# One SBUF ring with large tapering loads, fp32 exp in place and one activation table set in a log-sum-exp kernel

## The chip, the cores and the metric

The kernel runs on one core of a Trainium2 chip. The metric is the device time of the program in microseconds (us), as the median of several runs. The profile of one execution gives a span, from the first to the last instruction; the device time of the same run is longer, by the time outside the span.

## The reference

```python
def setup_inputs():
    batch, seq, dim = 32, 512, 1024
    return {"x": np.random.randn(batch, seq, dim).astype(np.float32), "axis": -1}

def reference(x, axis):
    x_max = np.max(x, axis=axis, keepdims=True)
    return (x_max.squeeze(axis) + np.log(np.sum(np.exp(x - x_max), axis=axis))).astype(np.float32)
```

There are 16,384 rows of 1,024 fp32 numbers, 67.11 MB, and one result per row. Both kernels leave the maximum out, because for normally distributed numbers exp does not overflow. They put 128 consecutive rows on each of the 128 partitions. From here on a "row" is one row on every partition: 128 x 4 KB = 0.524 MB. There are 128 of them.

## The kernel before

Separate pools hold tiles of 4, 2 and 1 rows. ScalarE makes bf16 exponentials in a second tile and VectorE sums them. Some rows are "fused": ScalarE writes exp and its accumulator gives the sum, without VectorE.

```python
SCHEDULE = [(4, 24), (2, 8), (1, 16)]      # rows per tile, number of tiles: 48 loads
N_TAIL_FUSED = 4
X_BUFS = {4: 4, 2: 4, 1: 6}
E_BUFS = {4: 3, 2: 3, 1: 4}
SCALAR_FUSE_EVERY = 2
# ... cut: pools, views ...
            xt = xpools[r].tile([P, r, D], fp32, name=f"xt{r}")
            nc.sync.dma_start(out=xt, in_=x_views[r][t])                 # L75
            if r == 1 and m0 >= NB - N_TAIL_FUSED:
                nc.scalar.activation(out=xt[:, 0], in_=xt[:, 0], func=Exp,
                                     accum_out=sums[:, m0 : m0 + 1])     # L78
            else:
                # ... cut: one fused row (L91) in every second tile of 4 ...
                et = epools[r].tile([P, r, D], bf16, name=f"et{r}")
                nc.scalar.activation(out=et[:, j0:r], in_=xt[:, j0:r], func=Exp)   # L98
                nc.vector.reduce_sum(out=sums[:, m0 + j0 : m0 + r],
                                     in_=et[:, j0:r], axis=mybir.AxisListType.X)   # L99
# ... cut ...
    nc.scalar.activation(out=res, in_=sums, func=Ln)                     # L107
    nc.scalar.dma_start(out=out_v, in_=res)
```

The softmax here doesn't subtract the row's maximum and nothing guards it: scores larger than these inputs give would overflow.

Of the kernel before, what the change touches and what calls it, by code (L numbers as in the profile page):

```python
# [1 line left out]

# [4 lines left out]


SCHEDULE = [(4, 24), (2, 8), (1, 16)]  # L10
N_TAIL_FUSED = 4
X_BUFS = {4: 4, 2: 4, 1: 6}
E_BUFS = {4: 3, 2: 3, 1: 4}
SCALAR_FUSE_EVERY = 2


@with_exitstack
def kernel(
    ctx: ExitStack,
    tc: tile.TileContext,  # L20
    x: bass.AP,
    axis: bass.AP,
    out: bass.AP,
):
    nc = tc.nc
    P = nc.NUM_PARTITIONS

    assert axis in (-1, len(x.shape) - 1), f"only last-axis reduction supported, got {axis}"

    x_flat = x.flatten_outer_dims()  # L30
    N, D = x_flat.shape
    assert N % P == 0
    NB = N // P

    fp32 = mybir.dt.float32
    bf16 = mybir.dt.bfloat16
    Exp = mybir.ActivationFunctionType.Exp
    Ln = mybir.ActivationFunctionType.Ln

    assert sum(r * c for r, c in SCHEDULE) == NB, "schedule must cover all blocks"  # L40

    out_v = bass.AP(
        tensor=out.tensor,
        offset=out.offset,
        ap=[[NB, P], [1, NB]],
    )

    sizes = sorted({r for r, _ in SCHEDULE})
    xpools = {}
    epools = {}  # L50
    for r in sizes:
        xpools[r] = ctx.enter_context(
            tc.tile_pool(name=f"xpool{r}", bufs=X_BUFS.get(r, 4))
        )
        epools[r] = ctx.enter_context(
            tc.tile_pool(name=f"epool{r}", bufs=E_BUFS.get(r, 4))
        )
    spool = ctx.enter_context(tc.tile_pool(name="spool", bufs=1))
    opool = ctx.enter_context(tc.tile_pool(name="opool", bufs=1))

    sums = spool.tile([P, NB], fp32)

    x_views = {
        r: x_flat.rearrange("(p t j) d -> t p j d", p=P, t=NB // r, j=r) for r in sizes
    }

    block = 0
    big_tile_idx = 0
    for r, count in SCHEDULE:
        for _ in range(count):  # L70
            m0 = block
            t = m0 // r
            assert m0 % r == 0
            xt = xpools[r].tile([P, r, D], fp32, name=f"xt{r}")
            nc.sync.dma_start(out=xt, in_=x_views[r][t])  # L75

            if r == 1 and m0 >= NB - N_TAIL_FUSED:
                nc.scalar.activation(  # L78
                    out=xt[:, 0],
                    in_=xt[:, 0],  # L80
                    func=Exp,
                    accum_out=sums[:, m0 : m0 + 1],
                )
            else:
                j0 = 0
                if r >= 4:
                    fuse_one = (big_tile_idx % SCALAR_FUSE_EVERY) == 0
                    big_tile_idx += 1
                    if fuse_one:
                        j0 = 1  # L90
                        nc.scalar.activation(  # L91
                            out=xt[:, 0],
                            in_=xt[:, 0],
                            func=Exp,
                            accum_out=sums[:, m0 : m0 + 1],
                        )
                et = epools[r].tile([P, r, D], bf16, name=f"et{r}")
                nc.scalar.activation(out=et[:, j0:r], in_=xt[:, j0:r], func=Exp)  # L98
                nc.vector.reduce_sum(  # L99
                    out=sums[:, m0 + j0 : m0 + r],  # L100
                    in_=et[:, j0:r],
                    axis=mybir.AxisListType.X,
                )
            block += r

    res = opool.tile([P, NB], fp32)
    nc.scalar.activation(out=res, in_=sums, func=Ln)  # L107
    nc.scalar.dma_start(out=out_v, in_=res)


# [1 line left out]
_INS = ['x', 'axis']  # L112
_OUTS = [((32, 512), 'float32')]
#: Inputs that are plain numbers.
_NUMBERS = {'axis': -1}


# [26 lines left out]
```

## Time and profile before

| quantity | before |
|---|---|
| device time on the first chip, median of 4 | 169.53 us (169.18 to 170.11) |
| device time on the three other chips, median of 7 each | 168.66, 168.59, 168.59 us |
| span of the profiled run | 166.7 us |
| loads of x | 48 |
| ScalarE / VectorE busy | 74% / 75% |
| last load landed / last Ln ended | 161.42 / 164.27 us |

The page of the profile begins with the busy time of the engines, then cuts the span into 40 slices, in tenths of busy time, and then gives the chain of work that ended last and the costliest groups:

```profile
span 166.7 us, 278 instructions
...
DVE 124.3 (75%) x44; ACT 124.0 (74%) x79; POOL 0.2 (0%) x4
...
DMA  5999999999999999999999999999999999999940
GB/s 193 440 433 436 429 413 433 436 433 429 421 421 436 436 433 429 405 436 436 433 429 409 436 436 433 429 417 425 425 415 425 425 411 418 409 409 409 407 186 16
...
q1 hardware_dynamic: 6912, 67.11, 95.9%
...
q14 instruction: 2, 0.02, 0.0%
...
DMA 78%; ACT 17%; SPq 2%; issue 1%; ACTq 0%
```

The DMA row is full from the second slice on, and 78% of the last chain are loads. Both compute engines are three quarters busy, but they wait for data. So the stream of loads is what has to become shorter.

The timeline of ScalarE shows the pace. Its columns are start, duration, engine, line, operation, output and input, shapes, count; the brackets hold the idle time before and what ended it. These are three tiles of 4 rows, then two of 1 row later on ("..." stands for lines left out):

```profile
32.57 3.62 ACT L98 ACTIVATE et<-xt 128x4096 bf16<-128x4096 f32 x1 [1.15 <-DMA xt<-in_x_dram]
37.40 1.06 ACT L91 ACTIVATE xt<-xt 128x1024 f32<-128x1024 f32 x1 [1.22 <-DMA xt<-in_x_dram]
...
42.36 3.62 ACT L98 ACTIVATE et<-xt 128x4096 bf16<-128x4096 f32 x1 [1.16 <-DMA xt<-in_x_dram]
...
151.26 1.06 ACT L98 ACTIVATE et<-xt 128x1024 bf16<-128x1024 f32 x1 [0.22 <-DMA xt<-in_x_dram]
152.54 1.06 ACT L98 ACTIVATE et<-xt 128x1024 bf16<-128x1024 f32 x1 [0.22 <-DMA xt<-in_x_dram]
```

ScalarE waits for every tile, so the distances are those of the loads: about 4.89 us for 4 rows, or 1.22 a row, and 1.28 for a single row. Small tiles cost more per row. (The landings in the trace give the line: 0.078 us per load plus 1.202 to 1.204 us per row.)

The end of the same timeline:

```profile
161.50 1.06 ACT L78 ACTIVATE xt<-xt 128x1024 f32<-128x1024 f32 x1
162.47 0.19 ACT L78 ACTIVATION_READ_ACCUMULATOR xt<-xt 128x1 f32 x1
162.67 1.28 ACT L107 ACT_TABLE_LOAD   x1
163.96 0.31 ACT L107 ACTIVATE res<-sums 128x128 f32<-128x128 f32 x1
164.30 0.37 ACTq L108 DMA_DIRECT2D out_dram<-res  x1
```

After the last load has landed (161.42, from the semaphore records of the trace) there are 2.85 us to the end of Ln. A table load of 1.28 us stands in them, because exp and Ln are taken from two table sets.

### The profile page before, as it was taken

To read this page: it belongs to the slowest core of one execution; us is meant where nothing else is said; L and a number is where in the kernel's file an instruction comes from. 1 tells how busy PE (TensorE), PEld (TensorE's weight loads), DVE (VectorE), ACT (ScalarE), POOL (GpSimd) and SP (SyncE) were. 2 spreads that over 40 slices of the span, in tenths; PEclk is the share of its full clock that TensorE was granted. 3 is DMA by queue.
4 is the path that set the end of the run, shared out by engine and by line. 5 is a ranking of instruction groups with operands and counts; after the bars stand their busy time and mean duration, and the time that the engine had idled before them with its cause. 6 is when DMAs were issued, how large, how long until landed. Compare 5 with 4: busy or idle time off the path is not lost.

```text
span 166.7 us, 278 instructions
## 1 busy us (share of the span) xinstructions
DVE 124.3 (75%) x44; ACT 124.0 (74%) x79; POOL 0.2 (0%) x4
## 2 busy tenths in 40 slices
DVE  0016986868798686879868687886869999999930
ACT  3088777778877777977777797777798787978894
POOL 0000000000000000000000000000000000000000
DMA  5999999999999999999999999999999999999940
GB/s 193 440 433 436 429 413 433 436 433 429 421 421 436 436 433 429 405 436 436 433 429 409 436 436 433 429 417 425 425 415 425 425 411 418 409 409 409 407 186 16
DMA packets 7058, 67.19 MB, mean 403 GB/s; under 512 B 784, under 2 KB 912, under 8 KB 2960
## 3 DMA queue, kind: packets, MB, share of 16 engines
q1 hardware_dynamic: 6912, 67.11, 95.9%
q10 hardware_dynamic: 144, 0.07, 0.1%
q14 instruction: 2, 0.02, 0.0%
HBM read 67.11 MB, written 0.07 MB: 403 GB/s over the span
## 4 chain that ended last, share of the span: by engine, by line
DMA 78%; ACT 17%; SPq 2%; issue 1%; ACTq 0%
DMA xt<-in_x_dram 78%; ACT et L98 16%; SPq L75 2%; ACT xt L78 1%; ACT L107 1%; ACT res L107 0%; ACTq L98 0%; ACTq L78 0%
## 5 line engine op out<-in xcount | busy, mean ns | idle before, releaser
L99 DVE TENSOR_REDUCE sums<-et 128x3 f32<-128x3072 bf16 (+3 forms) x44 | 124.3, 2863 | 35.5 <-ACT et L98 35.5
L98 ACT ACTIVATE et<-xt 128x3072 bf16<-128x3072 f32 (+3 forms) x44 | 103.9, 2369 | 19.5 <-DMA xt<-in_x_dram 19.2
L91 ACT ACTIVATE xt<-xt 128x1024 f32<-128x1024 f32 x12 | 12.7, 1056 | 19.5 <-DMA xt<-in_x_dram 19.5
L78 ACT ACTIVATE xt<-xt 128x1024 f32<-128x1024 f32 x4 | 4.2, 1056 | 0.5 <-DMA xt<-in_x_dram 0.2
L91 ACT ACTIVATION_READ_ACCUMULATOR xt<-xt 128x1 f32 x12 | 2.2, 187 | 0.0
L91 ACT ACT_TABLE_LOAD x1 | 1.3, 1283 | 0.7 <-PEq L125 0.7
L107 ACT ACT_TABLE_LOAD x1 | 1.3, 1283 | 0.0
L78 ACT ACTIVATION_READ_ACCUMULATOR xt<-xt 128x1 f32 x4 | 0.7, 186 | 0.0
L107 ACT ACTIVATE res<-sums 128x128 f32<-128x128 f32 x1 | 0.3, 309 | 0.0
L125 POOL MEMSET const-bfloat16-1.0<- 128x1 bf16 x1 | 0.1, 102 | 0.0
L125 POOL MEMSET const-uint8-127<- 128x1 uint8 x1 | 0.1, 102 | 0.0
L125 POOL MEMSET const-float32-0.0<- 128x1 f32 x1 | 0.1, 99 | 0.2 <-issue 0.2
L125 POOL MEMSET const-float32-1.0<- 128x1 f32 x1 | 0.1, 99 | 0.0
## 6 DMA issues: line engine op xcount, KB each, us to landing
xt<-in_x_dram SPq DMA_DIRECT2D x24, 2048.0 KB, 15.8
xt<-in_x_dram SPq DMA_DIRECT2D x8, 1024.0 KB, 13.0
xt<-in_x_dram SPq DMA_DIRECT2D x16, 512.0 KB, 6.6
out_dram<-res ACTq DMA_DIRECT2D x1, 64.0 KB, 1.6
```

What stands on the lines that cost most here:

```text
L75: nc.sync.dma_start(out=xt, in_=x_views[r][t])
L78: nc.scalar.activation(out=xt[:, 0], in_=xt[:, 0], func=Exp, accum_out=sums[:, m0 : m0 + 1],)
L91: nc.scalar.activation(out=xt[:, 0], in_=xt[:, 0], func=Exp, accum_out=sums[:, m0 : m0 + 1],)
L98: nc.scalar.activation(out=et[:, j0:r], in_=xt[:, j0:r], func=Exp)
L99: nc.vector.reduce_sum(out=sums[:, m0 + j0 : m0 + r], in_=et[:, j0:r], axis=mybir.AxisListType.X,)
L107: nc.scalar.activation(out=res, in_=sums, func=Ln)
L125: nc = _bacc.Bacc("TRN2", target_bir_lowering=False, num_devices=1)
```

## The change

The intent is to move the same bytes in fewer, larger loads, to drop the bf16 tiles so that there is room for one ring of 50 rows (200 KB on each partition), to divide the sums between ScalarE's accumulator and VectorE, and to take exp and Ln from one table set. The core of the diff, with cuts:

```diff
-SCHEDULE = [(4, 24), (2, 8), (1, 16)]
+CHUNKS = [                         # rows of the load, rows of it that VectorE sums
+    (12, 4), (14, 4), (16, 4), (16, 9), (16, 11), (12, 8), (10, 6), (8, 5),
+    (6, 4), (5, 3), (4, 2), (3, 1), (2, 0), (2, 0), (1, 0),
+]
+LAST_PARTS = [512, 512]
+RING_ROWS = 50
...
+    ring = pool.tile([P, RING_ROWS, D], fp32, name="ring")
+    nc.scalar.preload_act_table_set("natural_log_exp_and_others")
...
+    for r, n_dve in CHUNKS:
+        if slot + r > RING_ROWS:
+            slot = 0
+        nc.sync.dma_start(out=ring[:, slot : slot + r], in_=x_v[:, row : row + r])
+        if n_dve:
+            nc.scalar.activation(out=ring[:, slot : slot + n_dve],
+                                 in_=ring[:, slot : slot + n_dve], func=Exp)      # L60
+            nc.vector.reduce_sum(out=sums[:, row : row + n_dve],
+                                 in_=ring[:, slot : slot + n_dve], axis=AX)       # L63
+        for j in range(n_dve, r):
+            nc.scalar.activation(out=ring[:, slot + j], in_=ring[:, slot + j],
+                                 func=Exp, accum_out=sums[:, row + j : row + j + 1])  # L67
...
+    # last row: two loads of 512 columns, two fused halves (L84), after the first
+    # half Ln of the other 127 rows (L92), then a sum of the two parts on VectorE (L93)
+    # and Ln of one row (L94)
```

More of the change, by code (lines that the diff above doesn't have):

```diff
@@ L7 @@
 from concourse._compat import with_exitstack
-SCHEDULE = [(4, 24), (2, 8), (1, 16)]
-N_TAIL_FUSED = 4
-X_BUFS = {4: 4, 2: 4, 1: 6}
-E_BUFS = {4: 3, 2: 3, 1: 4}
-SCALAR_FUSE_EVERY = 2
+CHUNKS = [
[4 more added lines that the diff above has]
+RING_ROWS = 50
 @with_exitstack
@@ L33 @@
     NB = N // P
+    assert sum(r for r, _ in CHUNKS) + 1 == NB and sum(LAST_PARTS) == D
     fp32 = mybir.dt.float32
-    bf16 = mybir.dt.bfloat16
     Exp = mybir.ActivationFunctionType.Exp
     Ln = mybir.ActivationFunctionType.Ln
-    assert sum(r * c for r, c in SCHEDULE) == NB, "schedule must cover all blocks"
-    out_v = bass.AP(
-        tensor=out.tensor,
-        offset=out.offset,
-        ap=[[NB, P], [1, NB]],
-    )
-    sizes = sorted({r for r, _ in SCHEDULE})
-    xpools = {}
-    epools = {}
@@ L51 @@
-    for r in sizes:
-        xpools[r] = ctx.enter_context(
-            tc.tile_pool(name=f"xpool{r}", bufs=X_BUFS.get(r, 4))
-        )
-        epools[r] = ctx.enter_context(
-            tc.tile_pool(name=f"epool{r}", bufs=E_BUFS.get(r, 4))
-        )
-    spool = ctx.enter_context(tc.tile_pool(name="spool", bufs=1))
-    opool = ctx.enter_context(tc.tile_pool(name="opool", bufs=1))
-    sums = spool.tile([P, NB], fp32)
-    x_views = {
-        r: x_flat.rearrange("(p t j) d -> t p j d", p=P, t=NB // r, j=r) for r in sizes
-    }
@@ L67 @@
-    block = 0
-    big_tile_idx = 0
-    for r, count in SCHEDULE:
-        for _ in range(count):
-            m0 = block
-            t = m0 // r
-            assert m0 % r == 0
-            xt = xpools[r].tile([P, r, D], fp32, name=f"xt{r}")
-            nc.sync.dma_start(out=xt, in_=x_views[r][t])
-            if r == 1 and m0 >= NB - N_TAIL_FUSED:
-                nc.scalar.activation(
-                    out=xt[:, 0],
-                    in_=xt[:, 0],
-                    func=Exp,
-                    accum_out=sums[:, m0 : m0 + 1],
-                )
-            else:
-                j0 = 0
-                if r >= 4:
-                    fuse_one = (big_tile_idx % SCALAR_FUSE_EVERY) == 0
-                    big_tile_idx += 1
-                    if fuse_one:
-                        j0 = 1
-                        nc.scalar.activation(
-                            out=xt[:, 0],
-                            in_=xt[:, 0],
-                            func=Exp,
-                            accum_out=sums[:, m0 : m0 + 1],
-                        )
-                et = epools[r].tile([P, r, D], bf16, name=f"et{r}")
-                nc.scalar.activation(out=et[:, j0:r], in_=xt[:, j0:r], func=Exp)
-                nc.vector.reduce_sum(
-                    out=sums[:, m0 + j0 : m0 + r],
-                    in_=et[:, j0:r],
-                    axis=mybir.AxisListType.X,
-                )
-            block += r
@@ L106 @@
-    res = opool.tile([P, NB], fp32)
-    nc.scalar.activation(out=res, in_=sums, func=Ln)
+    AX = mybir.AxisListType.X
+    x_v = x_flat.rearrange("(p t) d -> p t d", p=P)
+    out_v = bass.AP(tensor=out.tensor, offset=out.offset, ap=[[NB, P], [1, NB]])
+    pool = ctx.enter_context(tc.tile_pool(name="pool", bufs=1))
+    ring = pool.tile([P, RING_ROWS, D], fp32, name="ring")
+    sums = pool.tile([P, NB], fp32, name="sums")
+    part = pool.tile([P, len(LAST_PARTS)], fp32, name="part")
+    res = pool.tile([P, NB], fp32, name="res")
@@ new lines @@
+    nc.scalar.preload_act_table_set("natural_log_exp_and_others")
+    row = slot = 0
+    for r, n_dve in CHUNKS:
[3 more added lines that the diff above has]
+        if n_dve:
+            nc.scalar.activation(
+                out=ring[:, slot : slot + n_dve], in_=ring[:, slot : slot + n_dve], func=Exp
+            )
+            nc.vector.reduce_sum(
+                out=sums[:, row : row + n_dve], in_=ring[:, slot : slot + n_dve], axis=AX
+            )
+        for j in range(n_dve, r):
+            nc.scalar.activation(
+                out=ring[:, slot + j],
+                in_=ring[:, slot + j],
+                func=Exp,
+                accum_out=sums[:, row + j : row + j + 1],
+            )
+        slot += r
+        row += r
@@ new lines @@
+    if slot + 1 > RING_ROWS:
+        slot = 0
+    c = 0
+    for k, w in enumerate(LAST_PARTS):
+        nc.sync.dma_start(out=ring[:, slot, c : c + w], in_=x_v[:, row, c : c + w])
+        c += w
+    c = 0
+    for k, w in enumerate(LAST_PARTS):
+        nc.scalar.activation(
+            out=ring[:, slot, c : c + w],
+            in_=ring[:, slot, c : c + w],
+            func=Exp,
+            accum_out=part[:, k : k + 1],
+        )
+        c += w
+        if k == 0:
+            nc.scalar.activation(out=res[:, 0:row], in_=sums[:, 0:row], func=Ln)
@@ L108 @@
+    nc.vector.reduce_sum(out=sums[:, row : row + 1], in_=part, axis=AX)
+    nc.scalar.activation(out=res[:, row : row + 1], in_=sums[:, row : row + 1], func=Ln)
     nc.scalar.dma_start(out=out_v, in_=res)
```

## The prediction

> **What bounds the kernel now: the load stream.** In the chain of waits that ended last, loads of x hold 78%, ScalarE 17%; ScalarE (74% busy) and VectorE (75%) wait for data. The page's DMA row is above 90% in every slice but the ends. The timeline of ScalarE gives the pace: 4-row tiles land every 4.894 us, 2-row tiles every 2.50, 1-row tiles every 1.282. One line fits: 0.078 us per load plus 1.204 us per row (0.524 MB), which is 435.5 GB/s; the Trainium skill ("DMA: Bandwidth & Descriptors", Where 436 GB/s comes from) has a ceiling of 435.2, so the trace agrees. The program: 1.85 us before the first byte, 128 x 1.204 = 154.1 us, 48 x 0.078 = 3.7 us, 1.25 us from last byte to semaphore; the last tile lands at about 161.5. Then a fused exp (1.06) with accumulator read (0.19), a table load (1.28), Ln 0.31, ending at 164.27; store and end 2.4: span 166.7. Measured 169.36, so 2.66 on top.
>
> **What the change does.**
> 1. 17 loads for 48: 31 x 0.078 = 2.4 us off the stream, all on the critical path. An estimate: it takes the fixed cost as per load (or per piece up to 64 KB). If pieces are cut again to 16 KB, about half is saved.
> 2. One table set: 1.28 us off the tail. Ln of 127 rows moves ahead of the last half row; a tiny VectorE reduce and a one-row Ln come at the end, 0.15 to 0.2 each with handoffs. Without backlog the path from last landing to last Ln falls from 2.8 to about 1.4 us.
> 3. ScalarE: 61 plain rows (0.853 a row plus about 0.11 an instruction) and 66 fused rows at 1.05 (start to start, as a fused row and its successor stand now): about 123 us, as now (124.0). VectorE falls from 124.3 to about 67 us, if fp32 reduces at the pace of bf16 (4096 in 4.42 us), as the skill ("VectorE: DVE Perf Modes", The perf-mode tier table) has it.
> 4. The ring. Walked by hand with these durations, each load's rows are free 3 us or more before the queue runs dry (tightest: the 8-row load behind the 11-row reduce): no gap. But a load is usable only when all of it has landed: ScalarE starts at 17.5 instead of 8.1 us, has no slack from the sixth load on, and in the last rows, mostly fused, trails the loads by about 1 us. That gives back much of step 2.
>
> Sum: last landing 158.4, last Ln 161.6, span 164.0, time **166.6 us** (-1.6%), range **164.8 to 168.4**. Faster by over 2%: 0.33; within 2%: 0.63; slower: 0.04.
>
> **What would show it.** Step 1: last load lands near 158.4; no slice of the middle under 425 GB/s. Step 2: one table load; 1.3 to 1.6 us from the last half row's exp to the last Ln's end. Step 3: fused rows start every 1.05 us; 4-row reduces still 4.4 us. Step 4: ScalarE idle 15.6 us before the first load, almost never after 107 us; the chain's last 15 us are ScalarE's, not loads.
>
> **What would make it wrong.** Fused rows back to back may cost 1.15 to 1.24, not 1.05: 1.5 to 4 us more. Long pieces may be slower than the fit. Or the stream is quicker or ScalarE level with it at the end: 165 us.

## More of the kernel before

The experiments ran on three chips, each beside its own runs of the kernel before. The chip on which the pair of kernels was first timed is not named in the record; it is called the first chip here, and the others the three other chips.

## The result, and the profile after

| | before | after |
|---|---|---|
| device time, first chip, median of 4 each | 169.53 us | 166.55 us (166.31 to 166.73) |
| ratio, first chip | | 0.9834 (95%: 0.9803 to 0.9865) |
| ratio, second and third chip on which both ran | | 0.9883 and 0.9877 |
| span of the profiled run | 166.7 us | 164.9 us |
| last load landed | 161.42 us | 159.53 us |
| last landing to the end of Ln | 2.85 us | 2.92 us |

Ratios are the mean time of one kernel's fast runs over that of the other's fast runs of the same rounds, so they are not quite the ratios of the medians. Results were correct in all experiments.

The page of the changed kernel, the lines that answer to those of before:

```profile
span 164.9 us, 255 instructions
...
DVE 67.1 (41%) x13; ACT 125.7 (76%) x151; POOL 0.2 (0%) x4
...
DMA  6998999997997998999899898999999999999940
...
q1 hardware_dynamic: 2448, 67.11, 95.3%
...
q14 instruction: 1, 0.01, 0.0%
...
DMA 54%; ACT 32%; DVE 8%; another core or an unknown queue 3%; issue 1%; SPq 0%; ACTq 0%
```

The packets on the load queue fall from 6,912 to 2,448, while the bytes stay the same. One packet moves one contiguous piece of one partition: a load is 128 pieces, 8 for each of the 16 DMA engines, and 16 packets of 4 bytes for its semaphore. The slices are now uneven: a packet of 64 KB takes 2.42 us, more than half a slice. ScalarE is as busy as before and has twice the share of the chain.

The groups, kept apart by shape (busy us, mean ns, then idle time before); the last line is from the kernel before:

```profile
L67 ACT ACTIVATE ring<-ring 128x1024 f32<-128x1024 f32 x66 | 68.7, 1043 | 0.0
L63 DVE TENSOR_REDUCE sums<-ring 128x4 f32<-128x4096 f32 x4 | 17.7, 4420 | 50.7 <-ACT ring L60 50.7
L60 ACT ACTIVATE ring<-ring 128x4096 f32<-128x4096 f32 x4 | 14.5, 3614 | 26.8 <-DMA ring<-in_x_dram 26.8
...
L99 DVE TENSOR_REDUCE sums<-et 128x4 f32<-128x4096 bf16 x12 | 53.0, 4419 | 16.9 <-ACT et L98 16.9
```

The fp32 reduce of 4 rows takes 4.420 us; the bf16 one of before took 4.419. The queue's own waits (us in total, times, longest):

```profile
SPq L58 <- DVE sums L63: 77.2, 5, 21.6
```

The queue waits long for rows of the ring, but always well ahead of need: no slice of the DMA row is empty in the middle, and no load after the first takes more than 0.31 us over the line above.

The last pieces of the chain (start, duration, what), and the end of the timeline:

```profile
124.21 24.09 DMA ring<-in_x_dram
...
148.38 1.91 ACT ring L60
150.30 2.08 ACT ring L67 x4
152.38 0.94 ACT ring L60
153.32 4.97 ACT ring L67 x9
```

```profile
159.46 1.05 ACT L67 ACTIVATE ring<-ring 128x1024 f32<-128x1024 f32 x1
...
160.50 0.63 ACT L84 ACTIVATE ring<-ring 128x512 f32<-128x512 f32 x1
...
161.11 0.31 ACT L92 ACTIVATE res<-sums 128x127 f32<-128x127 f32 x1
161.31 0.63 ACT L84 ACTIVATE ring<-ring 128x512 f32<-128x512 f32 x1
...
162.06 0.15 DVE L93 TENSOR_REDUCE sums<-part 128x1 f32<-128x2 f32 x1 [7.48 <-ACT ring L84]
162.25 0.20 ACT L94 ACTIVATE res<-sums 128x1 f32<-128x1 f32 x1 [0.22 <-DVE sums L93]
```

From 148.38 on the chain holds no load. The last load landed at 159.53, yet its half row is begun at 161.31: ScalarE is 1.8 us behind. The table load is gone, and the distance from last landing to the end of Ln is as long as it was.

### The profile page after: what moved, and what is told of

It is laid out like the page before. It is cut to its first block, busy times and chain, and to the rows that moved or that the text cites. A ratio compares the mean times of both kernels' runs of the same rounds, so it can differ in the third digit from the quotient of the medians.

```text
span 164.9 us, 255 instructions
## 1 busy us (share of the span) xinstructions
DVE 67.1 (41%) x13; ACT 125.7 (76%) x151; POOL 0.2 (0%) x4
## 3 DMA queue, kind: packets, MB, share of 16 engines
q1 hardware_dynamic: 2448, 67.11, 95.3%
## 4 chain that ended last, share of the span: by engine, by line
DMA 54%; ACT 32%; DVE 8%; another core or an unknown queue 3%; issue 1%; SPq 0%; ACTq 0%
DMA ring<-in_x_dram 54%; ACT ring L60 16%; ACT ring L67 15%; DVE sums L63 8%; ACT ring L84 1%; SPq L58 0%; ACT res L94 0%; ACT res L92 0%; DVE sums L93 0%; ACTq L60 0%; ACTq L92 0%
## 5 line engine op out<-in xcount | busy, mean ns | idle before, releaser
L63 DVE TENSOR_REDUCE sums<-ring 128x4 f32<-128x4096 f32 (+8 forms) x12 | 66.9, 5576 | 87.7 <-ACT ring L60 87.7
L60 ACT ACTIVATE ring<-ring 128x4096 f32<-128x4096 f32 (+8 forms) x12 | 54.5, 4539 | 35.8 <-DMA ring<-in_x_dram 35.7
L67 ACT ACTIVATE ring<-ring 128x1024 f32<-128x1024 f32 x66 | 68.7, 1043 | 0.0
L67 ACT ACTIVATION_READ_ACCUMULATOR ring<-ring 128x1 f32 x66 | 12.5, 190 | 0.0
L52 ACT ACT_TABLE_LOAD x1 | 1.3, 1283 | 0.7 <-PEq L112 0.7
L84 ACT ACTIVATE ring<-ring 128x512 f32<-128x512 f32 x2 | 1.3, 628 | 0.0
L84 ACT ACTIVATION_READ_ACCUMULATOR ring<-ring 128x1 f32 x2 | 0.4, 202 | 0.0
```

What stands on the lines that cost most here:

```text
L52: nc.scalar.preload_act_table_set("natural_log_exp_and_others")
L60: nc.scalar.activation(out=ring[:, slot : slot + n_dve], in_=ring[:, slot : slot + n_dve], func=Exp)
L63: nc.vector.reduce_sum(out=sums[:, row : row + n_dve], in_=ring[:, slot : slot + n_dve], axis=AX)
L67: nc.scalar.activation(out=ring[:, slot + j], in_=ring[:, slot + j], func=Exp, accum_out=sums[:, row + j : row + j + 1],)
L84: nc.scalar.activation(out=ring[:, slot, c : c + w], in_=ring[:, slot, c : c + w], func=Exp, accum_out=part[:, k : k + 1],)
```

## The experiments

Two questions were open after the result. What shortened the stream: fewer loads, or longer contiguous pieces? And why did the tail gain nothing though 1.28 us were taken out of it? There was also a discrepancy of bookkeeping: the prediction had added 2.66 us to the span, and the changed kernel showed 1.8.

### The table set alone

```diff
 # in the kernel before
     sums = spool.tile([P, NB], fp32)
+    nc.scalar.preload_act_table_set("natural_log_exp_and_others")
```

> The kernel before, with the shared exp-and-log table set loaded at the start and nothing else changed. Theory: the second table load (1.28 us) stands alone between the last row and Ln, so the span falls by 1.28 us to about 165.4, and the time by the same 1.3 us to about 168.2. Rival: the time outside the span is not a constant. Before it was 2.7 us (169.36 less 166.7), after it is 1.8 (166.69 less 164.9). If the second table set is what costs that 0.9 us outside the span, the time falls by about 2.2 us, to 167.3, with the span falling by 1.28 only.

Measured: 167.43 us against 168.66 on the same chip, ratio 0.9919 (0.9901 to 0.9936). The end of its timeline:

```profile
162.65 0.19 ACT L79 ACTIVATION_READ_ACCUMULATOR xt<-xt 128x1 f32 x1
162.87 0.31 ACT L108 ACTIVATE res<-sums 128x128 f32<-128x128 f32 x1
```

Ln follows the accumulator read directly. The gain is 1.2 us, the table load's own 1.28 within the scatter. The rival falls: in this run and in the runs of the kernel before beside it, time and span differ by 1.72 to 1.81 us, with one table set as with two. So the 2.66 us most likely came from a time and a span that did not belong together: the span of before, 166.67, plus 1.78 makes 168.45 us, which lies among the single runs on the other three chips (168.41 to 169.01), while the times beside it were 169.2 and more. It is not shown, because the record lists no span for those runs.

### Short pieces in few loads, and many short loads

```diff
 # e2: the changed kernel, 32 bytes left free after every row of the ring
-    ring = pool.tile([P, RING_ROWS, D], fp32, name="ring")
+    ring_padded = pool.tile([P, RING_ROWS, D + 8], fp32, name="ring")
+    ring = ring_padded[:, :, 0:D]

 # e3: the changed kernel, one load per row
-        nc.sync.dma_start(out=ring[:, slot : slot + r], in_=x_v[:, row : row + r])
+        for i in range(r):
+            nc.sync.dma_start(out=ring[:, slot + i], in_=x_v[:, row + i])
```

> The changed kernel with 32 unused bytes after each row of the ring, so that each of the same 17 loads is made of 4 KB pieces (1024 elements) instead of pieces of up to 64 KB. Theory A, the fixed cost goes with the contiguous piece: as costly as 128 loads of one row, 111 x 0.078 = 8.7 us more, about 175 us, every packet of 4 KB taking about 160 ns. Theory B, it goes with the load (its semaphore writes, its issue): no change, 166.5 us.

> The changed kernel with one load per row (129 loads) into the same contiguous ring; compute unchanged. Both theories of the fixed cost give a stream that is about 8.7 us longer, 128 rows at 1.28 us, the last landing at about 167.5. Compared with the run with short pieces in few loads: the difference is what the load itself costs (112 more loads); if the piece is all, the two land alike within 1 us. ScalarE, which then gets rows one at a time and more slowly than it works, should trail the last landing by under 1.6 us to the last Ln, so about 174 us.

| | loads | pieces of at most | time | ratio to before | last landing |
|---|---|---|---|---|---|
| changed kernel | 17 | 64 KB | 166.55 us (first chip) | 0.9834 | 159.53 us |
| short pieces | 17 | 4 KB | 173.48 us | 1.0278 | 166.37 us |
| row loads | 129 | 4 KB | 173.76 us | 1.0295 | 167.23 us |

The queues of the run with short pieces:

```profile
q1 hardware_dynamic: 16784, 67.11, 97.6%
```

With the same 17 loads, cutting the pieces to 4 KB moves the last landing by 6.8 us (7.0 against the later traces of the changed kernel, which landed at 159.33 and 159.36; it did not run on this chip). With the same pieces, 112 more loads move it by 0.9 us more, in one trace of each. So most of the fixed cost belongs to the contiguous piece: each of the 16 DMA engines gets 8 pieces per load in the kernel before, and 896 more pieces per engine in the padded run cost 6.8 us, 7.6 ns each. The packets say the same: those of 4 KB take 159 ns, those of 64 KB 2,420 ns, and 16 x 159 = 2,544, or 8 ns more per piece. A load itself costs about 0.008 us of stream. The padding itself is not the cause: the row loads have no padding, and in the experiment with loads cut to four rows (below), also without padding, 168 more pieces per engine in 21 more loads cost 1.29 us, 7.7 ns a piece with the load's share in it. Theory B is refuted. The 31 loads that the change saves are 248 pieces per engine, so by these figures 1.9 us for the pieces and 0.2 for the loads. The expected 8.7 us was too much; it took the 0.078 us of the line for the pieces alone and the first large loads to be on the line.

The tail of the row loads is telling too. There the loads come more slowly than ScalarE works, and 1.75 us pass from the last landing (167.23) to the end of Ln (168.98), in place of 2.92. That is more than the expected 1.6, but the lag is nearly gone.

### The last row whole

```diff
 # the changed kernel
-    # two loads, two fused halves, Ln of 127 rows between, sum of two parts, Ln of one row
+    nc.sync.dma_start(out=ring[:, slot], in_=x_v[:, row])
+    nc.scalar.activation(out=ring[:, slot], in_=ring[:, slot], func=Exp,
+                         accum_out=sums[:, row : row + 1])
+    nc.scalar.activation(out=res, in_=sums, func=Ln)
```

> The changed kernel with the last row loaded and processed whole, one Ln over all 128 sums at the end, no VectorE reduce of two parts. Theory (ScalarE is behind at the end, the loads are not what the end waits for): the split's second accumulator read, the handoff to VectorE and the one-row Ln are pure cost on ScalarE's own chain, 162.45 less 160.50 = 1.95 us now against about 1.04 + 0.25 + 0.31 = 1.6, so 0.3 us faster, about 166.2. Rival (the end waits for the last landing): the split brings the last Ln forward, undoing it costs about 0.5 us, 167.0.

It took 165.92 us (ratio 0.9831), but the changed kernel itself had not run on that chip. Both were therefore run again side by side on another:

> The changed kernel unaltered, on the same chip as the three runs beside it, since two chips gave the kernel before 169.5 and 168.7 us. Its ratio to the kernel before was 0.9834; 0.981 to 0.986 here. Last landing about 159.5, last Ln about 2.9 us later.

> The changed kernel with the last row whole and one Ln at the end, on the same chip as the changed kernel. Theory (the end waits for ScalarE): 0.4 to 0.6 us faster than the changed kernel beside it, as the spans of two chips had it (164.2 against 164.9). Rival (those were two chips): no difference, or slower.

The changed kernel took 166.57 us, the variant 166.05 us. Undoing the split is faster by 0.4 to 0.5 us (means 166.58 and 166.14), with the last landing where it was (159.33 and 159.29). The end of the variant's timeline:

```profile
160.31 1.04 ACT L78 ACTIVATE ring<-ring 128x1024 f32<-128x1024 f32 x1
...
161.48 0.31 ACT L84 ACTIVATE res<-sums 128x128 f32<-128x128 f32 x1
```

ScalarE begins the last row 1.0 us after it has landed. So a split that was made to hide the last piece of work behind the last load costs time when the engine that does it is already late: it only adds an accumulator read, a handoff and a second Ln.

The expected ratio of the changed kernel, 0.981 to 0.986, was missed: 0.9883 here. The changed kernel is as fast as on the first chip (166.55); the kernel before is not (168.59 in place of 169.53).

### Four rows from ScalarE to VectorE

```diff
 # the changed kernel: the last loads
-    (6, 4), (5, 3), (4, 2), (3, 1), (2, 0), (2, 0), (1, 0),
+    (6, 4), (5, 3), (4, 3), (3, 2), (2, 1), (2, 1), (1, 0),
```

> The changed kernel with four of the last rows, one in each of the loads of 4, 3, 2 and 2 rows, moved from the fused form (1.04 us of ScalarE) to plain exp with the sum on VectorE (0.85 to 0.96 us of ScalarE). Loads are as they were. Theory (ScalarE trails the loads at the end, so each 0.1 us taken from it comes off the time): worked out with the measured durations, last Ln 0.4 to 0.5 us earlier. Rival (the last landing or the store sets the end): no difference.

It took 166.22 us against 166.57, 0.35 us less, a little under what was expected (0.4 to 0.5). The last landing was at 159.44 us, and the end of Ln came 2.45 us after it (159.33 and 2.92 in the changed kernel beside it). The loads were not touched, so this supports the theory that ScalarE's lag sets the end.

### ScalarE level with the loads

```diff
 # the variant with the whole last row: the loads after the fifth
-    (12, 4), (14, 4), (16, 4), (16, 9), (16, 11), (12, 8), (10, 6), (8, 5),
-    (6, 4), (5, 3), (4, 2), (3, 1), (2, 0), (2, 0), (1, 0),
+    (12, 4), (14, 4), (16, 4), (16, 9), (16, 11), (11, 9), (10, 7), (7, 4),
+    (7, 5), (5, 4), (4, 2), (3, 2), (2, 2), (2, 2), (1, 0), (1, 0),
```

> The same first five loads, the rest cut anew (11, 10, 7, 7, 5, 4, 3, 2, 2, 1, 1 and one whole last row) with more rows summed on VectorE, so that by the measured durations ScalarE is level with the loads when the last one lands; one Ln at the end. Theory: from last landing to last Ln 1.6 us instead of 2.9, last landing unchanged (159.4), time 1.3 us below the changed kernel beside it, about 2.4% faster than the kernel before. If the stream of loads suffers from the finer end, the last landing moves by 0.08 us for each added load, no more.

> The level variant again, on a third chip: 1.2 us below the changed kernel beside it, about 165.4.

It took 165.39 us beside 166.57 for the changed kernel, and on a third chip 165.46 beside 166.46: 1.2 and 1.0 us less, where 1.3 and 1.2 were expected. Ratios to before: 0.9814 (0.9798 to 0.9829) and 0.9818. The expected 2.4% below the kernel before is 1.9%, because that kernel took 168.6 us here. This variant changes three things at once: 8 more rows go to VectorE, the loads from the sixth on are cut anew, and the last row is whole. The end of its timeline (first run):

```profile
158.55 1.04 ACT L66 ACTIVATE ring<-ring 128x1024 f32<-128x1024 f32 x1
...
159.59 1.04 ACT L78 ACTIVATE ring<-ring 128x1024 f32<-128x1024 f32 x1
160.54 0.19 ACT L78 ACTIVATION_READ_ACCUMULATOR ring<-ring 128x1 f32 x1
160.75 0.31 ACT L84 ACTIVATE res<-sums 128x128 f32<-128x128 f32 x1
```

The last load landed at 159.47 and ScalarE began its row at 159.59. Ln ended 1.59 us after the landing, as expected. This is the fastest of the kernels tried, 0.7% below the changed kernel.

### Loads cut to four rows

```diff
 # the changed kernel
-        nc.sync.dma_start(out=ring[:, slot : slot + r], in_=x_v[:, row : row + r])
+        for i in range(0, r, 4):
+            m = min(4, r - i)
+            nc.sync.dma_start(out=ring[:, slot + i : slot + i + m],
+                              in_=x_v[:, row + i : row + i + m])
```

> The changed kernel unaltered, reference for the runs beside it. 166.4 to 166.7 us, as on the chips so far; the ratio to the kernel before between 0.983 and 0.988, depending on the chip.

> The changed kernel with every load cut to at most 4 rows (38 loads instead of 17), ring, arithmetic and order as they were: the load part of the change undone to the size of before. The 8 pieces an engine gets per load cost 0.069 us by the run with short pieces, the load itself 0.01: 21 loads make 1.5 to 1.7 us, so the last landing is at about 161. ScalarE has 1.6 us more time for the same work and gets its rows sooner, so it trails less: last landing to last Ln 1.7 to 2.3 us instead of 2.9, time 0.5 to 1.0 us above the changed kernel beside it. If large loads are not what shortened the stream, the last landing stays at 159.4.

The changed kernel took 166.46 us (ratio 0.9877), the cut one 167.62 us (0.9946). The last landing moved from 159.36 to 160.65, 1.3 us for 21 loads, 0.06 a load, a little less than expected. Loads of more than 4 rows are thus worth 1.2 us of time (0.5 to 1.0 was expected). The second half of the expectation failed: the lag did not shrink. Ln ended 2.88 us after the last landing, as it does without the cut. The timeline shows why. ScalarE waited for the last load of 4 rows in both (it began on it at 148.23 in the changed kernel beside it, at 149.48 here) and never again, and the loads after it are the same in both kernels:

```profile
149.48 1.91 ACT L64 ACTIVATE ring<-ring 128x2048 f32<-128x2048 f32 x1 [0.53 <-DMA ring<-in_x_dram]
```

The lag is thus made in the last seven loads alone, from that one on: each load is at least as large as the next, so the 4 us that ScalarE needs for 4 rows meet the 3.7 us in which 3 rows arrive, and so on.

### Large loads halved

```diff
 # the level variant: loads of 14 and 16 rows in two halves
+        half = r if r < 14 else r // 2
+        for i in range(0, r, half):
+            nc.sync.dma_start(out=ring[:, slot + i : slot + i + half],
+                              in_=x_v[:, row + i : row + i + half])
```

> The level variant with its four loads of 14 and 16 rows issued as two halves each. In the trace of the changed kernel those four took 0.06, 0.31, 0.12 and 0.23 us more than the line 0.078 + 1.202 a row that all smaller loads keep. If that excess belongs to the size, halves lose 0.7 and pay 4 x 0.078: last landing 0.4 us earlier than the level variant beside it. If it is chance or belongs to the place in the program, 0.3 us later.

It took 165.85 us against 165.46 for the level variant beside it, and the last landing came at 159.96 instead of 159.41, 0.55 us later. So the excess of the large loads is not a property of their size. In the level variant the three loads of 16 rows took 19.35 us each, 0.04 over the line, and in halves 19.42 us at the least. What remains over the expected 0.3 us is mostly one load of 8 rows that landed 0.23 us over the line (at 54.75). A later load of 7 rows was late in both runs, by 0.49 us here and by 0.40 in the level variant; after it the slowest of the 16 DMA engines was 0.47 and 0.37 us behind the next. The cause of such delays was not found.

## Why the prediction was right, point by point

The predicted time, 166.6 us, is the measured 166.55. Its sum, however, held two errors that cancel: the span was to be 164.0 and is 164.9 us, and the time outside it was to be 2.66 and is 1.8 us. That the two met to 0.05 us is luck. The 0.9 us of the span are a last landing that came 1.1 us later than predicted, less a tail (last landing to the end of Ln) that was 0.3 us shorter than its sum had it (2.92 for 3.2). Going by the span, the change was to save 2.7 us and saves 1.8.

- **The stream is the bound: right.** The last landing came 1.89 us earlier and the span fell by 1.76.
- **Step 1, 17 loads for 48, 2.4 us off: the mechanism right, the gain too large.** The cost belongs to the piece, and pieces of 64 KB stay whole (2,448 packets for 17 loads: 128 of data and 16 for the semaphore each). But 1.9 us came off, not 2.4, and the last load landed at 159.53, not at 158.4. The terms that were too small: the first load landed at 18.12 instead of the 17.63 that these terms give (1.85 + 12 x 1.204 + 0.078 + 1.25), because the 16 DMA engines begin one after another, from 1.73 to 2.56 us, and their first packets take 0.6 to 1.0 us longer than later ones; and the four loads of 14 and 16 rows took 0.7 us over the line in all (0.2 and 0.4 in the two later traces of the same kernel, so this part varies from run to run). The prediction's sum for the kernel before was off too: its terms give 160.9 for the last landing, not the 161.5 that stands there. 161.42 was measured, with two late loads of 0.46 and 0.16 us in it. So the saving of 2.4 us and the landing at 158.4, 3.1 us earlier, did not agree with each other. The test "no slice of the middle under 425 GB/s" failed (318 to 511) and was a bad one: packets are too long for the slices, and the kernel before has slices of 405 too.
- **Step 2, one table set: right, the check a little off.** There is one table load. Alone in the kernel before it brings 1.2 us. From the start of the last half row's exp to the end of the last Ln there are 1.14 us (161.31 to 162.45), less than the predicted 1.3 to 1.6.
- **Step 3, durations: right.** Fused rows start every 1.04 us (predicted 1.05), the fp32 reduce takes as long as the bf16 one, ScalarE is busy for 125.7 us (predicted about 123) and VectorE for 67.1 (67).
- **Step 4, the ring holds and ScalarE trails: right, and stronger.** No gap in the stream; ScalarE was idle for 16.1 us before the first load and for 1.5 us in all after 107 us; the chain's last 14 us are its own. ScalarE trails by 1.8 us, not by about 1. The lag takes back not "much of step 2" but all of it: 2.85 us of tail before, 2.92 after. (The prediction's numbers had that already: 158.4 to 161.6 is a tail of 3.2 us. Its words and its sum differ.) Three experiments that give ScalarE less to do at the end, the last also with other load sizes, bring 0.35, 0.4 to 0.5 and 1.0 to 1.2 us, with the last landing within 0.15 us of where it was.
- **The end of the sum, 2.66 us outside the span: wrong.** It is 1.72 to 1.84 in every run that lists both. The time and the span of before that were subtracted most likely did not belong to one run. Why the kernel before took 169.5 us on the first chip and 168.6 on three others is open; the record lists no span for the longer times. On the two of those chips on which both kernels ran, the change is worth 1.2%, not 1.7%.

The parts also add up. The level variant keeps both gains, 1.95 us of stream and 1.26 us of tail (2.85 to 1.59), and is 3.2 us faster than the kernel before beside it (168.59 to 165.39).

## What to carry to other kernels

When a stream of loads is the bound, make the contiguous pieces on each partition long (here about 0.06 us for the 8 pieces that an engine gets per load); how many loads they are issued in matters far less (0.008 us a load). When loads taper, check the engine that consumes them against each next load, not against the average: here a saving of 1.3 us at the end was lost whole to an engine that was 76% busy. And subtract a span only from the time of the same run.

## What the Trainium skill lacked or had wrong

- "DMA: Bandwidth & Descriptors", Rules for kernel authors: for the highest bandwidth it asks for 128 partitions and at least 1 MiB per DMA. Loads of 8 MB made of 4 KB pieces took 20.33 us per 16 rows (412.6 GB/s), those made of 64 KB pieces 19.35 us (433.5 GB/s). What counts beyond 1 MiB is the contiguous piece, at about 8 ns each in these runs; the page has no time per piece for pieces of 4 to 64 KB. The page's section on small descriptors gives a cost of about 3 cycles per packet and its table of specifications has 512 bytes as the least for line rate. Its port ceiling of 435.2 GB/s agrees with the slope of 1.202 us a row, which is 436 GB/s; the page, though, has that ceiling bind transfers within SBUF and has the HBM side, at about 358 GB/s, bind loads from HBM, and here one core loaded 403 and 407 GB/s over the whole span.
- "ScalarE: Activation LUTs", What ACT_TABLE_LOAD costs: 1,283 ns for the load agrees (1,283 in the trace), but the further 1,380 ns for a drain were not seen. The load began as the accumulator read ended (162.66), Ln began as the load ended, and leaving the load out saved 1.2 us in all.
- "ScalarE: Activation LUTs", the same section: an ACTIVATE of 1,024 elements with constant scale and bias at 186 + 853 ns agrees (1,038 to 1,057; these kernels give no scale or bias). The cost of the accumulator is missing: its read is listed with 190 ns, but fused rows follow each other every 1.04 us, where plain ones by the page's overlap of 93 ns would every 0.95 (an estimate; the changed kernel's one plain row with a successor right behind it took 0.947 from start to start), so it adds about 0.09 us.
- "VectorE: DVE Perf Modes", The perf-mode tier table: a reduce runs at the same pace in bf16 and fp32; agrees, 4.419 and 4.420 us for 4,096 elements.
- "Runtime: NRT & Kernel Launch", Instruction fetch mechanics: it calls the fetch of the program's next instructions "mostly hidden". The page does not say what it does to a stream of loads on the same DMA engines. The instruction queue moved two packets of 8 KB during the kernel before (at 124.3 and 155.1 us) and one during the changed kernel (58.6 us), about 0.31 us each. In the kernel before, the load in flight each time landed 0.46 and 0.16 us later than its size asks for, because a load is complete only when its slowest engine is. It came again with such packets in the run with the table set alone (0.19 and 0.25 us) and in the run with loads of four rows (0.38). But in the second run of the level variant the load in flight with the packet was on the line (0.04), and in other runs a lag came without a packet of this kind, so this is a coincidence in time that was not tested.
